# A two-layer hybrid mixer on one core: the scheduler orders the engines by its plain instruction model in place of a played time line

## The chip, the core and the metric

The kernel runs on one core of a Trainium2 chip. The core has five engines that work at the same time, each through its own list of instructions in the order in which the list stands: TensorE (PE; its weight loads are shown apart as PEld), VectorE (DVE), ScalarE (ACT), GpSimd (POOL) and SyncE (SP), which here issues all transfers. An instruction that needs another engine's result waits for a semaphore, and everything behind it on its engine waits with it. The metric is the device time of one execution in microseconds, less is better.

## The reference

Two layers over 1024 latent and 256 context tokens of width 1024. Each layer projects the normed tokens with one wide matrix into the inputs of three mixers, runs the mixers, and projects their outputs back:

```python
h = rms_norm(x) * (1 + scale[:, None]) + shift[:, None]
hc = rms_norm(ctx) * (1 + scale_c) + shift_c
aq, ak, av, ag, xbc, dtr, z, rq, rk, rv, rg = split_columns(h @ w_in, IN_SPLITS)
...
q_l = apply_rope(attn_heads(aq, attn_q_norm), cos, sin)
k_l = apply_rope(attn_heads(ak, attn_k_norm), cos, sin)
...
s = jnp.einsum('bqhmd,bkhmd->bhmqk', q, k).astype(jnp.float32) * (ATT_QK_DIM ** -0.5)
p = jax.nn.softmax(s, axis=-1)
a = p[:, :, 0] - lam * p[:, :, 1]
...
ys_l, _, _ = bidirectional_scan(cm_l, bm_l, vf_l, vb_l, laf_l, lab_l, ssd_sf, ssd_sb, True)
yr_l, _, _ = bidirectional_scan(q_rl, k_rl, v_rl, v_rl, lf_rl, lb_rl, ret_sf, ret_sb, True)
...
mix = jnp.concatenate([attn_lat, ssd_lat, ret_lat], axis=-1).astype(x.dtype)
x_new = x + gate[:, None] * (mix @ w_out)
```

The mixers are differential attention (4 heads, two softmaxes each), a state-space scan in both directions (16 heads) and a retention scan in both directions (4 heads). The last layer gives the latent tokens alone.

## The kernel before

**The work.** Tokens lie in three chunks (512, 512, 256). Each product with a projection matrix is taken in three parts (high times high, high times low, low times high) of numbers that ACT rounds (L282) and DVE or POOL subtracts (L284). Such a product over the depth of 1024 is a group of 24 matmuls into one bank of PSUM: `t_group` at L310 (weights first) or `dense_n` at L312 (tokens first). These dense groups are the filler of the kernel. The mixers are the rest: `dt_chunk` makes the time steps of the scan for a chunk of tokens (PE's L578, L625 to L628 and L648, with DVE, ACT and POOL between them), `pair_prep` and `pair_phase` run the scan for two heads at a time (L766, L772, L793 to L834), `pair_end` gates a pair (POOL's L895, ACT's L897), `head_prep` norms and rotates the queries and keys of a head, `head_loop` runs its attention, one iteration for 128 queries, and `ret_mix` is the retention.

**The rope.** `qk_norm` ends with a product on DVE (L942) and one on POOL (L943). `rope` then works in two halves: POOL multiplies by the sines (L924) into a side tile rm, DVE multiplies by the cosines in place (L925), so it must not begin before POOL has read, and adds the crossed terms (L928, L929):

```python
nc.gpsimd.tensor_tensor(out=m, in0=x4, in1=sb, op=ALU.mult)
nc.vector.tensor_tensor(out=x4, in0=x4, in1=cb, op=ALU.mult)
```

**An iteration of attention.** `head_b` makes the scores s of one softmax on PE (L986, two matmuls a chunk of keys, three chunks), their maxima mx on DVE (L988, and nb over the three at L993), and the exponentials e with their sums z on ACT (L998). It runs twice. `head_c1` adds up z (zs, L1007), takes its reciprocal (rz, L1011) and the ratio rho (L1013), and subtracts the second softmax from the first in place (e, L1016). PE transposes the result (L149, t<-ident,e), DVE or ACT copies it out (aT, L118 or L116), and PE multiplies by v (L1037). The scores have three banks of PSUM, so a score pair waits until the exponential of the pair three before it has been read.

**What sets the order.** The Python code writes the instructions down in one sequence. Generators mix the mixers' steps and the dense groups: `pump` takes one step of the stream of dense groups, `phase` does so between two steps of a mixer until a budget (`SHARE`) is used. That sequence is only a preference. On leaving the `TileContext`, its scheduler plays the program against a model of the chip, and at each moment gives an engine the earliest written instruction among those that are ready by the model. What comes out is the fixed list of each engine, with the semaphores. Which matmul fills the gap until a transpose is ready is thus decided by how long the model thinks that the engines between take. The argument `schedule_with_timeline_sim` picks the model.

## Time and profile before

| | |
|---|---|
| median of 3 runs | 2871.17 us (2867.28 to 2872.06) |
| the profiled execution | 2869.1 us |
| its span, first to last instruction | 2867.3 us |
| PE busy | 2665.5 us, 17116 matmuls |
| DVE, ACT, POOL busy | 1781.3, 1056.4, 772.1 us |
| mean granted clock of TensorE | 0.964 |
| the chain that ended last | PE 76%, DVE 12%, ACT 3% of the span |

Busy time is that of an engine's own instructions; the rest of the span it waits or has nothing to do. The chain is followed back from the last instruction, at each step to what released it. The granted clock is a share of TensorE's full 2.4 GHz; the chip grants this or half of it.

### The profile page before, as it was taken

How to read it: one execution, taken by the hardware profiler on the slowest of the kernel's cores; microseconds unless marked ns; L12 is line 12 of the kernel's file. 1: busy time of each engine (PE TensorE's matmuls, PEld its weight loads, DVE VectorE, ACT ScalarE, POOL GpSimd, SP SyncE). 2: the span in 40 equal slices, each digit the busy share in tenths (PEclk: the TensorE clock that was granted, in tenths of full speed). 3: DMA queues.
4: the chain of work that ended last, by engine and by line, in shares of the span. 5: the costliest groups of instructions: out<-in, count | busy, mean ns of one | idle time of the engine just before them, and what ended most of it. 6: DMA issues, size and time to landing. Idle time of an engine off the chain costs nothing.

```text
span 2867.3 us, 45100 instructions
## 1 busy us (share of the span) xinstructions
PE 2665.5 (93%) x17116; PEld 2339.0 (82%) x17116; DVE 1781.3 (62%) x4213; ACT 1056.4 (37%) x2678; POOL 772.1 (27%) x688
## 2 busy tenths in 40 slices
PE   6799999999999999989989989999999999999999
PEld 4578877888888899977878777878988888889787
DVE  5567767656677766565435566667676767564651
ACT  3443333224454545341223443332254444442330
POOL 2333223232111121243331423223421221022540
PEclk9899999999999999998999999999999999999999
DMA  6021212222111111033452112112210010002461
GB/s 244 10 62 62 67 44 83 70 69 89 45 54 45 54 31 39 27 110 109 136 179 95 36 41 72 53 50 65 60 30 16 23 30 23 23 17 66 139 209 55
DMA packets 111832, 196.04 MB, mean 68 GB/s; under 512 B 13600, under 2 KB 43104, under 8 KB 111616
## 3 DMA queue, kind: packets, MB, share of 16 engines
q1 hardware_dynamic: 111616, 193.17, 21.3%
q8 instruction: 135, 2.21, 0.3%
q14 instruction: 81, 0.66, 0.1%
HBM read 155.43 MB, written 37.68 MB: 67 GB/s over the span
## 4 chain that ended last, share of the span: by engine, by line
PE 76%; DVE 12%; ACT 3%; issue 2%; DMA 2%; POOL 1%; SPq 0%; DVEq 0%; ACTq 0%; POOLq 0%
PE mm L310 34%; PE mm L312 18%; PE t L149 5%; PE o L1037 4%; PE s L986 4%; PE s L772 2%; PE s L822 2%; DVE mx L988 2%; PE o L815 2%; PE t L793 1%; ACT e L998 1%; DVE e L1016 1%; DMA mr<-mix 1%; DVE rs L1156 1%; PE s L1146 1%
## 5 line engine op out<-in xcount | busy, mean ns | idle before, releaser
L310 PE MATMUL mm<-ah,wh 128*128 128x512 f32 (+1 forms) x1680 | 629.4, 375 | 30.1 <-DVE xr L1223 13.8
L310 PE MATMUL mm<-al,wh 128*128 128x512 f32 (+1 forms) x1680 | 622.8, 371 | 1.5 <-DVE al L284 0.9
L310 PE MATMUL mm<-ah,wl 128*128 128x512 f32 (+1 forms) x1680 | 622.4, 371 | 0.6 <-POOL wl L284 0.6
L284 POOL TENSOR_TENSOR wl<-raw,wh 128x512 fp32r<-128x512 f32 x224 | 294.5, 1335 | 769.5 <-ACT wh L282 736.9
L312 PE MATMUL mm<-wh,ah 128*128 128x256 f32 x1568 | 455.7, 291 | 9.5 <-DVE q L118 7.0
L312 PE MATMUL mm<-wl,ah 128*128 128x256 f32 x1568 | 450.4, 287 | 0.0
L312 PE MATMUL mm<-wh,al 128*128 128x256 f32 x1568 | 448.7, 286 | 0.0
L310 PEld LDWEIGHTS mm<-ah,wh 128*128 128x128 f32 x1680 | 322.3, 192 | 85.8 <-issue 13.8
L310 PEld LDWEIGHTS mm<-al,wh 128*128 128x128 f32 x1680 | 322.2, 192 | 51.1 <-issue 1.4
L310 PEld LDWEIGHTS mm<-ah,wl 128*128 128x128 f32 x1680 | 321.2, 191 | 51.2 <-POOL wl L284 1.1
L312 PEld LDWEIGHTS mm<-wh,ah 128*128 128x128 f32 x1568 | 302.5, 193 | 16.6 <-DVE q L118 7.7
L998 ACT ACTIVATE e<-s,nb 128x512 f32<-128x512 f32 (+1 forms) x384 | 231.7, 613 | 206.2 <-DVE nb L993 203.6
L312 PEld LDWEIGHTS mm<-wl,ah 128*128 128x128 f32 x1568 | 302.7, 193 | 2.4 <-POOL wl L284 0.2
L312 PEld LDWEIGHTS mm<-wh,al 128*128 128x128 f32 x1568 | 302.3, 193 | 2.2 <-issue 0.2
L988 DVE TENSOR_REDUCE mx<-s 128x1 f32<-128x512 f32 (+1 forms) x400 | 225.1, 589 | 55.4 <-PE s L986 53.2
L986 PE MATMUL s<-kT,qT 128*128 128x512 f32 (+1 forms) x800 | 215.8, 375 | 17.0 <-ACT e L998 15.5
L282 ACT ACTIVATE wh<-raw 128x512 fp32r<-128x512 f32 x224 | 130.0, 625 | 226.2 <-PE mm L310 103.9
L1037 PE MATMUL o<-v,aT 128*128 128x128 f32 x1312 | 174.9, 276 | 0.0
L986 PEld LDWEIGHTS s<-kT,qT 128*128 128x128 f32 x800 | 134.3, 193 | 41.3 <-ACT e L998 26.5
L1037 PEld LDWEIGHTS o<-v,aT 128*128 128x128 f32 x1312 | 163.8, 193 | 4.1 <-DVE v L118 0.8
L794 ACT ACTIVATE t<-t 128x512 f32<-128x512 f32 x144 | 82.2, 582 | 146.5 <-PE t L793 142.5
L766 POOL TENSOR_TENSOR xw<-xn,dtpk 128x512 f32<-128x512 f32 (+2 forms) x96 | 79.4, 838 | 208.9 <-PE s L772 93.5
(282 smaller groups left out, 4544.5 us busy)
## 6 DMA issues: line engine op xcount, KB each, us to landing
raw<-in_wi_dram SPq DMA_DIRECT2D x176, 256.0 KB
wa<-in_wa_dram SPq DMA_DIRECT2D x48, 512.0 KB
E<-cume SPq DMA_DIRECT2D x144, 128.0 KB
mr<-mix SPq DMA_DIRECT2D x64, 256.0 KB
raw<-in_wo_dram SPq DMA_DIRECT2D x32, 256.0 KB
x<-xr SPq DMA_DIRECT2D x26, 256.0 KB
mix<-cv SPq DMA_DIRECT2D x8, 640.0 KB
mix<-sg SPq DMA_DIRECT2D x8, 640.0 KB
```

The lines of the kernel that those rows point to most:

```text
L149: self.nc.tensor.transpose(ps[:, j * P:(j + 1) * P], srcs[i + j], self.ident)
L282: nc.scalar.activation(out=hi, in_=x, func=AF.Copy)
L284: e.tensor_tensor(out=lo, in0=x, in1=hi.bitcast(F32), op=ALU.subtract)
L310: nc.tensor.matmul(ps, lhsT=w, rhs=x, start=st, stop=sp)
L312: nc.tensor.matmul(ps, lhsT=x, rhs=w, start=st, stop=sp)
L766: nc.gpsimd.tensor_tensor(out=xw, in0=xn[:, a:a + m].rearrange("p t (h e) -> p t h e", h=2), in1=self.wend[:, a:a + m, h0:h0 + 2].unsqueez ...
L772: nc.tensor.matmul(ps[:, j * P:(j + 1) * P], lhsT=bn[:, c, :], rhs=xw[:, j].rearrange("p h e -> p (h e)"), start=True, stop=True)
L794: nc.scalar.activation(out=ps, in_=ps, func=AF.Exp)
L986: nc.tensor.matmul(ps[:, 0:n], lhsT=qT[:, 2 * m + s, :], rhs=kT[m][:, t0:t0 + n], start=(s == 0), stop=(s == 1))
L988: nc.vector.tensor_reduce(out=mx[:, ci:ci + 1], in_=ps[:, 0:n], axis=AX.X, op=ALU.max, negate=len(chunks) == 1)
L998: nc.scalar.activation(out=em[:, t0:t0 + n], in_=pss[ci][:, 0:n], func=AF.Exp, bias=nb, accum_out=z[:, 3 * m + ci:3 * m + ci + 1])
L1037: nc.tensor.matmul(po[:, 0:P], lhsT=aT[j], rhs=v[:, j, :], start=(j == b0), stop=(j == NT - 1))
```

## The change

```diff
-    with _tile.TileContext(nc, schedule_with_timeline_sim=True) as tc:
+    with _tile.TileContext(nc, schedule_with_timeline_sim=False) as tc:
```

The program that goes in is the same, and so is every instruction that comes out; only their order on each engine and the semaphores between them differ. PE's list has 12287 rows before and 12322 after, where equal neighbours are merged, and nearly all of it is shifted a little. Three places follow. Names carry the number of the tile, so that the same tile can be found in both.

The first place is on DVE, in the second head of the first layer, where the queries of the next head are rotated (q2_1212_7414) while an iteration of attention runs (s_1453_8512 and its neighbours are scores, e_1422_8357 the exponentials that the transposes wait for). Before:

```order
L942 TENSOR_TENSOR q2_1212_7414<-q2_1212_7414,ry_1414_8327 128x1280
L1007 TENSOR_REDUCE zs_1458_8530<-z_1416_8341 128x2
L1011 RECIPROCAL rz_1459_8532<-zs_1458_8530 128x2
L1013 SCALAR_TENSOR_TENSOR rho_1460_8534<-zs_1458_8530,nlam0_280,rz_1459_8532 128x1
L1016 SCALAR_TENSOR_TENSOR e_1422_8357<-e_1445_8455,rho_1460_8534,e_1422_8357 128x1280
L118 COPY v3_1429_8383<-mm_1461_8537 128x128
L988 TENSOR_REDUCE mx_1452_8511<-s_1453_8512 128x1
L988 TENSOR_REDUCE mx_1452_8511<-s_1454_8516 128x1
L988 TENSOR_REDUCE mx_1452_8511<-s_1455_8520 128x1
L993 TENSOR_REDUCE nb_1456_8524<-mx_1452_8511 128x1
L925 TENSOR_TENSOR q2_1212_7414<-q2_1212_7414,cos_338 128x512
L118 COPY v3_1429_8383<-mm_1477_8612 128x128
```

After:

```order
L942 TENSOR_TENSOR q2_1212_7414<-q2_1212_7414,ry_1414_8327 128x1280
L993 TENSOR_REDUCE nb_1444_8453<-mx_1440_8440 128x1
L1038 TENSOR_SCALAR O_1195_7358<-o_1447_8486,rz_1424_8363 128x128
L988 TENSOR_REDUCE mx_1452_8511<-s_1453_8512 128x1
L925 TENSOR_TENSOR q2_1212_7414<-q2_1212_7414,cos_338 128x512 x2
L928 TENSOR_TENSOR q2_1212_7414<-q2_1212_7414,rm_1449_8500 128x8x32
L929 TENSOR_TENSOR q2_1212_7414<-q2_1212_7414,rm_1449_8500 128x8x32
L928 TENSOR_TENSOR q2_1212_7414<-q2_1212_7414,rm_1450_8505 128x8x32
L929 TENSOR_TENSOR q2_1212_7414<-q2_1212_7414,rm_1450_8505 128x8x32
L988 TENSOR_REDUCE mx_1452_8511<-s_1454_8516 128x1
L988 TENSOR_REDUCE mx_1452_8511<-s_1455_8520 128x1
L1007 TENSOR_REDUCE zs_1458_8530<-z_1416_8341 128x2
```

Both products by the cosines (L925) and the four L928 and L929 have moved ahead of two of the three maxima (L988); nb, the ratio rho and e follow behind the maxima, where before e stood ahead of all of this.

The second place is on PE, an iteration later: the transposes of e_1457_8526 (t_1488_8695). Rows of L312 are dense matmuls. Before, the score s_1495_8715 stands 23 dense matmuls and another score ahead of the transposes; these are the last rows ahead of them:

```order
L312 MATMUL mm_1508_8780<-wh_1397_8272,al_111_567 128x256
L986 MATMUL s_1502_8764<-kT_991_6388,qT_1469_8586 128x256 x2
L312 MATMUL mm_1508_8780<-wh_1397_8272,ah_110_566 128x256
L312 MATMUL mm_1508_8780<-wl_1398_8273,ah_110_566 128x256
L312 MATMUL mm_1508_8780<-wh_1397_8272,al_111_567 128x256
L312 MATMUL mm_1508_8780<-wh_1397_8272,ah_110_566 128x256
L312 MATMUL mm_1508_8780<-wl_1398_8273,ah_110_566 128x256
L312 MATMUL mm_1508_8780<-wh_1397_8272,al_111_567 128x256
L312 MATMUL mm_1508_8780<-wh_1397_8272,ah_110_566 128x256
L149 MATMUL t_1488_8695<-ident_87,e_1457_8526 128x128 x4
```

After, from that score on:

```order
L986 MATMUL s_1495_8715<-kT_1026_6530,qT_1438_8433 128x256 x2
L312 MATMUL mm_1499_8735<-wh_1397_8272,ah_110_566 128x256
L312 MATMUL mm_1499_8735<-wl_1398_8273,ah_110_566 128x256
L312 MATMUL mm_1499_8735<-wh_1397_8272,al_111_567 128x256
L312 MATMUL mm_1499_8735<-wh_1397_8272,ah_110_566 128x256
L312 MATMUL mm_1499_8735<-wl_1398_8273,ah_110_566 128x256
L312 MATMUL mm_1499_8735<-wh_1397_8272,al_111_567 128x256
L312 MATMUL mm_1499_8735<-wh_1397_8272,ah_110_566 128x256
L312 MATMUL mm_1499_8735<-wl_1398_8273,ah_110_566 128x256
L149 MATMUL t_1488_8695<-ident_87,e_1457_8526 128x128 x4
L149 MATMUL t_1490_8702<-ident_87,e_1457_8526 128x128 x4
```

The transposes have moved up to 8 dense matmuls behind the score s_1495_8715, and the score s_1502_8764 has moved behind them.

The third place is on PE at the start of the layer, where the log decays la_174_1104 of the third chunk come from POOL (L617). Between the transposes of L578 that begin this chunk's time steps and L625, which reads la, 81 dense matmuls stand before and 44 after; in the other five chunks it is 72 to 91 before and 34 to 49 after. The last rows after the change:

```order
L310 MATMUL mm_182_1139<-ah_149_858,wl_65_352 128x256
L310 MATMUL mm_182_1139<-ah_149_858,wh_64_351 128x256
L310 MATMUL mm_182_1139<-al_150_859,wh_64_351 128x256
L625 MATMUL s_175_1109<-la_174_1104,uf_341 128x32
L626 MATMUL s_175_1109<-la_174_1104,ub_342 128x32
L628 MATMUL t_176_1112<-la_174_1104,ones_89 128x64
L310 MATMUL mm_182_1139<-ah_149_858,wl_65_352 128x256
L310 MATMUL mm_182_1139<-ah_149_858,wh_64_351 128x256
```

L625 has moved from the middle of a later dense group (mm_195_1216) into the group mm_182_1139.

## Rows read from the trace of the kernel before

**Rows 1.** Page, part 1: busy time, share of the span, instructions.
```profile
PE 2665.5 (93%) x17116; PEld 2339.0 (82%) x17116; DVE 1781.3 (62%) x4213; ACT 1056.4 (37%) x2678; POOL 772.1 (27%) x688
```

**Rows 2.** Cores: span and mean granted clock of TensorE.
```profile
core 0: 2867.3 us, clock 0.964
```

**Rows 3.** PE's waits: what waits, for what; us in total, times, longest.
```profile
PE s L986 <- ACT e L998: 15.5, 15, 2.2
...
PE t L149 <- DVE khl L284: 11.1, 10, 2.9
PE t L149 <- DVE cv L512: 7.8, 4, 2.4
PE t L149 <- DVE e L1016: 7.4, 6, 2.1
PE t L793 <- DVE mt L796: 7.4, 6, 2.3
PE s L772 <- POOL xw L766: 7.2, 5, 2.4
```

**Rows 4.** A stretch of attention by windows: us busy of each engine (x instructions).
```profile
800.00:900.00 100.00, 92.83 (x715) 85.32 (x713) 78.84 (x187) 49.68 (x154) 17.79 (x10) 0.98 0.12 39
```

**Rows 5.** Timeline of DVE, 866 to 892 us: start, us, line, operation.
```profile
873.09 1.49 DVE L942 TENSOR_TENSOR q<-q,ry 128x1280 f32<-128x1280 f32 x1
...
874.89 2.81 DVE L1013 SCALAR_TENSOR_TENSOR rho<-zs,nlam,rz 128x1 f32<-128x1 f32 x1
877.74 2.66 DVE L1016 SCALAR_TENSOR_TENSOR e<-e,rho,e 128x1280 f32<-128x1280 f32 x1
...
880.52 1.60 DVE L988 TENSOR_REDUCE mx<-s 128x1 f32<-128x512 f32 x3
...
882.24 0.68 DVE L925 TENSOR_TENSOR q<-q,cos 128x512 f32<-128x512 f32 x1
...
883.63 0.41 DVE L928 TENSOR_TENSOR q<-q,rm 128x256 f32<-128x256 f32 x1
883.97 0.42 DVE L929 TENSOR_TENSOR q<-q,rm 128x256 f32<-128x256 f32 x1
...
890.79 0.22 DVE L1013 SCALAR_TENSOR_TENSOR rho<-zs,nlam,rz 128x1 f32<-128x1 f32 x1
891.05 1.55 DVE L1016 SCALAR_TENSOR_TENSOR e<-e,rho,e 128x1280 f32<-128x1280 f32 x1
```

**Rows 6.** Timeline of POOL, 864 to 900 us, all of its rows.
```profile
874.73 2.95 POOL L943 TENSOR_TENSOR q<-q,keep 128x1280 f32<-128x1280 f32 x1 [35.53 <-DVE zs L1007]
877.76 3.77 POOL L924 TENSOR_TENSOR rm<-q,sin 128x512 f32<-128x512 f32 x2
```

**Rows 7.** Timeline of ACT, 872 to 892 us.
```profile
889.01 0.68 ACT L998 ACTIVATE e<-s,nb 128x512 f32<-128x512 f32 x1
```

**Rows 8.** Timeline of PE, 875 to 896 us; idle time before in brackets.
```profile
879.08 0.28 PE L312 MATMUL mm<-wl,ah 128*128 128x256 f32 x1
879.20 0.28 PE L312 MATMUL mm<-wh,al 128*128 128x256 f32 x1
880.45 1.09 PE L149 MATMUL t<-ident,e 128*128 128x128 f32 x8 [0.98 <-DVE e L1016]
...
894.16 1.04 PE L149 MATMUL t<-ident,e 128*128 128x128 f32 x8
```

**Rows 9.** Line L924: ns least, median, most; first and last start.
```profile
L924 POOL TENSOR_TENSOR rm<-k,sin x16: 1266/1287/1343, 576.5 to 2359.7; 128x512 f32<-128x512 f32 x16
```

**Rows 10.** Line L1016, the same columns.
```profile
L1016 DVE SCALAR_TENSOR_TENSOR e<-e,rho,e x72: 476/1551/2668, 647.5 to 2559.1; 128x1280 f32<-128x1280 f32 x64, 128x256 f32<-128x256 f32 x8
```

**Rows 11.** Timeline of PE, 142.5 to 152.9 us.
```profile
144.91 0.28 PE L310 MATMUL mm<-al,wh 128*128 128x256 f32 x1
```

**Rows 12.** Timeline of POOL, 138 to 152 us.
```profile
147.41 0.34 POOL L617 TENSOR_TENSOR la<-dtw,keep 128x64 f32<-128x64 f32 x1
```

**Rows 13.** Line L895, columns as in rows 9.
```profile
L895 POOL TENSOR_TENSOR cv<-cv,zu x16: 2357/2902/3324, 228.7 to 2040.5; 128x1280 f32<-128x1280 f32 x8, 128x1024 f32<-128x1024 f32 x8
```

## Prediction

> **What bounds the kernel now.** I read the engines' shares first [rows 1]: TensorE is busy 2665.5 of 2867.3 us, 93%, so idle for 2867.3 - 2665.5 = 202 us. No other engine is near that, and the work is the same after the change, instruction for instruction. So the question is only whether PE's 202 us of idle time grow or shrink. Second comes the clock [rows 2]: the mean granted clock is 0.964, so 0.036 x 2867.3 = 103 us of PE's time is the price of stretches at 1.2 instead of 2.4 GHz; that is 103 / 202 = 0.51 us beside each idle us. I use it as a factor of 1.51 on every us that PE stands more or less, though not each short wait brings a slow stretch. Third, the list of PE's waits [rows 3]: the mixer's own waits, where a score, a transpose or a decay matmul stood a little too early, are the six largest that the order can move. They sum to 15.5 + 11.1 + 7.8 + 7.4 + 7.4 + 7.2 = 56 us over the whole kernel, so in the old order the filler matmuls cover nearly every chain. Last, a stretch of attention [rows 4]: PE is busy 93 of 100 us and DVE 79, so DVE is the second bound there, and it takes its instructions strictly as they stand.
>
> **What moves, and its price.** In the new PE order the mixer's matmuls stand earlier against the dense ones (L310, L312), and the dense ones stand together in whole groups of 24. I lay the new order on the old durations at three places and count them up.
>
> *The rope, first place (ordered rows of DVE above).* L925 needs POOL's L924, which needs POOL's L943, which needs DVE's L942. In the old order DVE does rho, e and three maxima (L1013, L1016, L988) between L942 and L925, and finds POOL ready. In the new order both L925 and the four L928/L929 stand right behind the first maximum, and behind them wait the other two maxima, nb, rho and e. L942 ends at 874.58 [rows 5]. POOL's L943 then takes 2.95 us, to 877.68; one L924 takes 1.29 (the median) [rows 6, 9], so the second one ends at about 880.3. L925 takes 0.68 [rows 5], four additions start 0.34 apart behind it, so DVE comes back to the maxima at about 882.3; two of them (three take 1.60 in [rows 5]) end at 883.4, and zs, a copy and nb, small ones like the 0.22 of L1013 that overlap in part, give nb at about 883.9, and the first exponential (0.68 [rows 7]) ends at 884.6. PE's next score pair waits for that one to free its bank (s_8594). Before them stand three score pairs, the last released by the third exponential of the pair before (its nb now stands right behind L942, and three exponentials of at most 0.68 that overlap end about 1.9 later, at 876.5), and 39 dense matmuls at 0.12 us each [rows 8], so PE is there at 876.9 + 4.7 = 881.6 and stands 3.0 us. The old order stood 0.98 us in that place [rows 8], so the net is 2.0. There are 16 such ropes in the attention heads (32 L924 on q and k, of which [rows 9] show the 16 on k; two in a rope): 16 x 2.0 = 32 us. Bounds: all 16 lose 3.0, 48 us; or none does and the 0.98 goes too, -16.
>
> At this place the old trace shows a second thing. L1013 makes one element for each partition and took 2.81 us, ending at 877.70 just when POOL's L943 ended (877.68); the same line took 0.22 us at 890.79, after the last of POOL's work in this stretch [rows 5, 6]. L1016 behind it took 2.66 instead of 1.55: together 3.7 us longer, more than the 3.0 that the new place costs. The Trainium skill ("SBUF — State Buffer", "Who interferes with whom") says that a VectorE instruction with two SBUF inputs shares an interface with GpSimd and that the second to issue waits for the whole of the first; the trace agrees. By that rule the new order gives back what the old one lost here, since DVE now stands still while POOL works, and the rope term would be 0 instead of 32. This is the second rival below.
>
> *The attention's transposes, second place (ordered rows of PE above).* t_8695 needs e_8526 from L1016. The old order has 23 dense matmuls and a score between s_8715 and it, and it started at 894.16 without a wait [rows 8]. The new one has 8 dense matmuls. s_8715 is released by the second exponential, at 889.01 + 0.68 = 889.7 [rows 7]; 0.24 us of score and 8 x 0.12 us later PE is there, at 890.9. e_8526 was ready at 891.05 + 1.55 = 892.6 [rows 5], so PE stands 1.7 us. L1016 runs 72 times [rows 10]. At the rope's place its transposes stand behind 39 dense matmuls and lose nothing of their own, so I take one iteration in four: 18 x 1.7 = 31 us, between 0 and 72 x 1.7 = 122.
>
> *The time steps of the state-space part (dt_chunk).* L625 needs POOL's L617. Between L578 and L625 stand 72 to 91 dense matmuls in the six chunks before, and 34 to 49 after; in the third chunk 81 and 44 (24 of one group and 20 of the next). The 44th ended at 144.91 + 0.28 = 145.2; L617 ended at 147.41 + 0.34 = 147.75 [rows 11, 12]. PE stands 2.6 us. Six chunks: 16 us, from 0 to 16, since the chunks differ in what covers them.
>
> *The gate's square (L897).* ACT waits there for POOL's L895, 2.9 us a time, 16 times [rows 13], and evacuations of dense groups (L485) now stand behind it. PE has up to a dense group in hand (24 matmuls, 2.9 us), so I take 1.0 us of the 2.9 each: 16 us, from 0 to 46.
>
> *What it gives back.* Groups of dense matmuls in one piece, and mixer chains that start sooner, take away part of the 56 us of [rows 3]: half, -28, from 0 to -56.
>
> Sum: 32 + 31 + 16 + 16 - 28 = 67 us, with the clock 67 x 1.51 = 101. The profiled execution took 2869.1 us (span 2867.3), 2 below the median of the three runs, so 2869.1 + 101 = **2970 us**.
>
> **The rivals.** *Every iteration waits.* If the tight place is in all 72 iterations, because DVE is at 79% and its head of line now blocks more, the second term is 122 instead of 31: 158 x 1.51 = 239, 3108 us. For it: [rows 4]; against it: the whole groups of 24 behind each cluster let the chain catch up.
>
> *The rope is free* (the shared interface, above): 35 x 1.51 = 53, 2922 us. For it the 2.81 us of [rows 5]; against it that not DVE's time counts but when nb comes, 883.9.
>
> *Faster.* The mixer's earlier places take away all of the 56 us, and DVE and ACT, whose orders move along with PE's, have the results there sooner than the old times say, so that of the losses only the time steps' 16 us stay: -40 x 1.51 = -60, 2809 us. It decides below 56 / 72 = 0.8 us for each L1016, all losses put together. For it: the chains by their bare durations fit the new gaps in most iterations; against it: both places that I worked out in attention miss by 1.7 to 3.0 us.
>
> *Nothing.* The moves are local, and groups of 24 matmuls (2.9 us) take up each loss: 2869 us within 6 us (0.2%, about what a measurement of this kernel tells from no change).
>
> **How the numbers follow.** Forecast 0.49, every iteration waits 0.20, free rope 0.17, faster 0.09, nothing 0.05. All but the last two are slower by over 0.2%: slower 0.86, same 0.05, faster 0.09. The likeliest case alone is 2923 to 3017 us (its first two terms at half and at one and a half times their size). The range of 8 in 10 takes in the free rope at 2922 with room for a smaller second term, 2885, and the case in which every iteration waits, 3108, 3120; what lies outside is the faster case, nothing, and the sum of all upper bounds.
>
> **What the new profile would show.** Right: PE's idle time near 270 us, not 202; L925 waiting for POOL L924 in the list of DVE's waits with 20 to 50 us, where the old trace has 1.5 us; PE's transposes of e (L149) waiting for L1016 with some 30 us instead of 7.4; L625 waiting for POOL la; and a mean clock near 0.95. Wrong: if L925 waits and PE's scores do not, the rope is free; if the clock stays at 0.964 while idle time grows, the factor 1.51 was wrong; if PE's largest new wait is on a DMA, or on a dense group's evacuation, the loss is one that I have not priced.

## The result and the profile after

The changed kernel takes 2912.51 us in the median of 4 runs (2908.22 to 2918.20), the kernel before 2870.86 in the same comparison: a ratio of 1.0149, 95% interval 1.0132 to 1.0167. It is 42 us slower. The prediction was 2970 us, 101 slower, in a range from 2885 to 3120.

The page of the kernel after (part 1), its cores view and its list of PE's waits (what waits, for what; us in total, times, longest):

```profile
PE 2696.2 (92%) x17116; PEld 2345.6 (80%) x17116; DVE 1767.3 (61%) x4213; ACT 1067.4 (37%) x2678; POOL 764.6 (26%) x688
```

```profile
core 0: 2916.4 us, clock 0.958
```

```profile
PE s L986 <- ACT e L998: 16.2, 7, 3.1
PE mm L312 <- DVE q L118: 14.4, 3, 6.4
PE t L149 <- DVE cv L512: 13.4, 6, 5.6
...
PE s L625 <- POOL la L617: 10.6, 3, 4.4
...
PE t L149 <- DVE sg L1099: 7.4, 2, 5.3
...
PE s L772 <- POOL xw L766: 4.7, 7, 2.1
...
PE t L149 <- DVE e L1016: 2.5, 2, 1.3
...
PE t L793 <- DVE mt L796: 2.0, 3, 1.0
...
PE t L149 <- DVE khl L284: 0.6, 1, 0.6
```

PE is idle for 2916.4 - 2696.2 = 220 us, where it was 202 [rows 1], and the clock takes (1 - 0.958) x 2916.4 = 122 us, where it took 103 [rows 2]. The profiled execution's 49 us (2916.4 - 2867.3) are thus 18 us of idle time, 19 us of slow clock and 12 us in which PE counts as busy at full speed for a little longer. (This execution is the slowest of the four; the others have a clock of 0.958 to 0.963, and the medians lie 42 us apart.) In the list of waits [rows 3], the transposes of e have fallen from 7.4 to 2.5 us and those of khl from 11.1 to 0.6; the scores stay at 16, but in 7 waits of up to 3.1 us instead of 15 of up to 2.2. What has grown are waits for L118, which empties banks of dense groups, and for L512 (7.8 before); the one for L1099 is new. The largest of L118 was 7.0 us before, in three waits as well:

```profile
PE mm L312 <- DVE q L118: 7.0, 3, 5.7
```

Where the time went is read at places at which both orders have done the same matmuls. The windows of the two kernels between such places (columns as in [rows 4]; the count of PE's matmuls tells that the work is the same within 2), before and then after:

```profile
0.00:555.40 555.40, 493.19 (x2923) 405.92 (x2924) 354.06 (x908) 198.53 (x383) 168.10 (x163) 0.93 0.24 79
555.40:666.50 111.10, 105.20 (x786) 95.27 (x785) 63.60 (x146) 35.79 (x91) 32.99 (x20) 0.97 0.28 91
666.50:1213.70 547.20, 522.40 (x3854) 478.09 (x3855) 376.41 (x906) 247.75 (x756) 105.37 (x78) 0.99 0.14 45
1213.70:1994.30 780.60, 718.82 (x4075) 613.53 (x4074) 465.31 (x1072) 251.58 (x526) 239.86 (x243) 0.94 0.28 86
1994.30:2075.50 81.20, 81.20 (x643) 77.44 (x642) 46.06 (x118) 24.42 (x58) 34.45 (x23) 1.00 0.21 63
2075.50:2548.00 472.50, 436.55 (x3074) 400.27 (x3072) 321.50 (x763) 222.12 (x669) 81.99 (x54) 0.98 0.08 24
2548.00:2867.30 319.30, 308.17 (x1770) 268.48 (x1770) 154.35 (x304) 76.18 (x197) 109.31 (x108) 0.99 0.33 106
```

```profile
0.00:547.90 547.90, 490.00 (x2923) 402.77 (x2924) 347.16 (x894) 199.59 (x383) 167.46 (x163) 0.93 0.25 81
547.90:673.80 125.90, 112.94 (x787) 101.41 (x786) 72.63 (x175) 36.12 (x91) 38.22 (x22) 0.91 0.24 80
673.80:1234.10 560.30, 531.60 (x3854) 480.90 (x3852) 368.00 (x891) 251.90 (x756) 94.89 (x77) 0.98 0.14 43
1234.10:2019.90 785.80, 723.34 (x4077) 607.29 (x4076) 450.09 (x1072) 254.46 (x527) 240.57 (x244) 0.96 0.28 86
2019.90:2116.00 96.10, 86.41 (x643) 81.12 (x642) 52.18 (x119) 23.21 (x56) 32.06 (x21) 0.95 0.16 48
2116.00:2567.40 451.40, 433.48 (x3076) 395.91 (x3075) 321.30 (x768) 226.06 (x674) 82.43 (x54) 0.98 0.09 26
2567.40:2916.40 349.00, 318.48 (x1770) 276.18 (x1768) 155.93 (x296) 76.05 (x194) 108.98 (x108) 0.96 0.30 97
```

The seven stretches are the start with the scan of the first layer, the preparation of its first attention head, its iterations of attention, the change of layers with the second scan, then head and iterations again, and the end (retention and projection). After minus before they are -7.5, **+14.8**, +13.1, +5.2, **+14.9**, -21.1 and **+29.7** us. PE's idle time (length minus busy time) moves by -4.3, +7.1, +3.9, +0.7, +9.7, -18.0 and +19.4. The iterations of attention, on which 63 of the prediction's 95 us of losses (before what it gives back) rested, come out 8 us shorter. The net loss lies at the three stretches, of 96 to 349 us, in which the work changes from one mixer to the next.

DVE and ACT waited as foreseen. The list of waits of DVE has L925 for L924 with 29.4 us (1.5 before, the last of the three lines), that of ACT L897 for L895 with 43.1 (11.8 before):

```profile
DVE q L925 <- POOL rm L924: 18.3, 7, 3.7
...
DVE k L925 <- POOL rm L924: 11.1, 4, 4.3
```

```profile
DVE q L925 <- POOL rm L924: 1.5, 1, 1.5
```

```profile
ACT zu L897 <- POOL cv L895: 43.1, 16, 4.3
```

### The profile page after: what moved, and what is told of

Its sections match the earlier page's. It is cut to its first block, busy times and chain, and to the rows that moved or that the text cites. A ratio compares the mean times of both kernels' runs of the same rounds, so it can differ in the third digit from the quotient of the medians.

```text
span 2916.4 us, 45079 instructions
## 1 busy us (share of the span) xinstructions
PE 2696.2 (92%) x17116; PEld 2345.6 (80%) x17116; DVE 1767.3 (61%) x4213; ACT 1067.4 (37%) x2678; POOL 764.6 (26%) x688
## 5 line engine op out<-in xcount | busy, mean ns | idle before, releaser
L310 PE MATMUL mm<-ah,wh 128*128 128x512 f32 (+1 forms) x1680 | 638.1, 380 | 31.5 <-DVE xr L1223 11.9
L310 PE MATMUL mm<-al,wh 128*128 128x512 f32 (+1 forms) x1680 | 631.5, 376 | 3.3 <-POOL al L284 2.9
L310 PE MATMUL mm<-ah,wl 128*128 128x512 f32 (+1 forms) x1680 | 629.2, 375 | 1.8 <-POOL wl L284 1.8
L284 POOL TENSOR_TENSOR wl<-raw,wh 128x512 fp32r<-128x512 f32 x224 | 297.6, 1348 | 1039.2 <-ACT wh L282 1038.5
L312 PE MATMUL mm<-wh,ah 128*128 128x256 f32 x1568 | 459.7, 293 | 32.4 <-DVE q L118 14.4
L312 PE MATMUL mm<-wl,ah 128*128 128x256 f32 x1568 | 453.0, 289 | 2.1 <-POOL wl L284 2.1
L312 PE MATMUL mm<-wh,al 128*128 128x256 f32 x1568 | 453.0, 289 | 0.0
L312 PEld LDWEIGHTS mm<-wh,ah 128*128 128x128 f32 x1568 | 307.3, 196 | 37.9 <-DVE q L118 15.0
L312 PEld LDWEIGHTS mm<-wl,ah 128*128 128x128 f32 x1568 | 307.6, 196 | 3.7 <-POOL wl L284 2.7
L312 PEld LDWEIGHTS mm<-wh,al 128*128 128x128 f32 x1568 | 307.2, 196 | 0.8 <-issue 0.2
L988 DVE TENSOR_REDUCE mx<-s 128x1 f32<-128x512 f32 (+1 forms) x400 | 225.7, 588 | 56.3 <-PE s L986 55.3
L986 PE MATMUL s<-kT,qT 128*128 128x512 f32 (+1 forms) x800 | 212.0, 380 | 16.6 <-ACT e L998 16.2
L986 PEld LDWEIGHTS s<-kT,qT 128*128 128x128 f32 x800 | 138.2, 196 | 43.1 <-ACT e L998 21.4
L1037 PE MATMUL o<-v,aT 128*128 128x128 f32 x1312 | 165.1, 275 | 0.0
L1037 PEld LDWEIGHTS o<-v,aT 128*128 128x128 f32 x1312 | 157.1, 192 | 2.4 <-ACT e L998 0.8
```

What stands on the lines that cost most here:

```text
L284: e.tensor_tensor(out=lo, in0=x, in1=hi.bitcast(F32), op=ALU.subtract)
L310: nc.tensor.matmul(ps, lhsT=w, rhs=x, start=st, stop=sp)
L312: nc.tensor.matmul(ps, lhsT=x, rhs=w, start=st, stop=sp)
L986: nc.tensor.matmul(ps[:, 0:n], lhsT=qT[:, 2 * m + s, :], rhs=kT[m][:, t0:t0 + n], start=(s == 0), stop=(s == 1))
L988: nc.vector.tensor_reduce(out=mx[:, ci:ci + 1], in_=ps[:, 0:n], axis=AX.X, op=ALU.max, negate=len(chunks) == 1)
L1037: nc.tensor.matmul(po[:, 0:P], lhsT=aT[j], rhs=v[:, j, :], start=(j == b0), stop=(j == NT - 1))
```

## The experiments

All kernels are made with one tool. The scheduler runs with its plain model, and each instruction of an engine is tied behind its predecessor in a written list by an ordering edge, which costs no semaphore. With the lists of the new order the program after comes out (all_new below); the old lists were not run alone, but the order on PE and ACT in the trace of old_rope_fwd is that of the kernel before. Any mixture of both can be run. Theory A is the prediction's own account, theory B the reading of the windows above; C and D, on what happens at the places, are told in the expectations that use them. Each kernel was timed beside the kernel before on its chip, but not all on one chip. Across chips the ratios to the kernel before are the safer comparison, and each holds to 4 to 7 us either way.

```diff
+def _pin(nc, tc):
...
+            if prev is not None and x:
+                tc.add_manual_dep(by[name], prev, mb.DependencyInfo(mb.DependencyClass.NoSync, mb.DependencyReason.DATA),
+                                  reason="pin")
...
-    with _tile.TileContext(nc, schedule_with_timeline_sim=True) as tc:
+    with _tile.TileContext(nc, schedule_with_timeline_sim=False) as tc:
         tile_hybrid_kernel(tc, args, out)
+        _pin(nc, tc)
```

**The yardstick: all lists new.**

> The new order of every engine, written out as pins: the kernel after, as a yardstick on the same chip for the other three. Every theory: 2912 within 6 us.

Measured 2913.55 us, ratio to before 1.0139 (1.0116 to 1.0163). The edges cost nothing that these runs can tell, and the 42 us come from the order alone.

### Which stretch loses

The lists change source at the places above ("until" in the time of the source's own profile):

```diff
+new_start: new until 548, then old
+new_entry: old until 555.4, new until 673.8, old until 1994.3, new until 2116, then old
+new_loop:  old until 666.5, new until 1234.1, old until 2075.5, new until 2567.4, then old
+new_rest:  old until 1213.7, new until 2019.9, old until 2548, then new
```

> The new order on all engines up to 548 us (its own time; start, conditioning, time steps and the first scan pairs), the old order from there on. Theory A (the prediction: dt_chunk and the gate's square cost in the scans): half of the 16 + 16 us of these terms, times 1.51, about +15 to +24 us. Theory B (read off the two traces by places where both orders have done the same matmuls: the loss sits in stretches where the work changes from one mixer to the next): -7 us here, 2864.

> The new order only in the two stretches in which the first attention head of a layer is prepared (548 to 674 and 2020 to 2116 us of the new trace), the old order elsewhere. Theory A: these stretches hold two or three of the 16 ropes and none of the iterations, so +5 us or less. Theory B: +14.8 + 14.9, about +30 us, 2900.

> The new order only in the iterations of attention (674 to 1234 and 2116 to 2567 us of the new trace), the old order elsewhere. Theory A: the ropes and the transposes of e are here, 63 us of idle time, 95 us with the clock; even scaled down to the loss that was measured it must be most of the 42 us, 2895 to 2965. Theory B: +13 - 21, about -8 us, 2863.

> The new order from the end of the first layer's attention to the second layer's last scan pair (1234 to 2020 us of the new trace) and from 2567 us to the end (retention, output projection), the old order elsewhere. Theory A: the other half of the time steps' and the gate's terms, +15 to +24 us, all of it before 2020 us. Theory B: +5 there and +30 from 2567 us to the end, about +35 us, 2906.

| | median, us (before 2870.58) | ratio, 95% interval | difference |
|---|---|---|---|
| new_start | 2861.27 | 0.9963 (0.9951 to 0.9976) | -9 |
| new_entry | 2903.85 | 1.0117 (1.0099 to 1.0135) | +33 |
| new_loop | 2859.84 | 0.9965 (0.9952 to 0.9979) | -11 |
| new_rest | 2912.67 | 1.0145 (1.0126 to 1.0163) | +42 |

Theory A falls: the iterations of attention are faster in the new order, and so are the start's time steps and scan. Theory B holds in sign at all four and in size within 7 us (new_rest has 42 instead of 35, with an interval that begins at 36). (The four add up to 55, 13 more than the whole loss; which of them has too much was not found out.)

### What loses there

At these stretches PE waits for a bank of PSUM, or for a transpose's input, that DVE has not come to yet. The clearest place is the retention's chain of states, 18 products (L1156), nine in each direction, each of which needs the one before it in its direction. In the old order two to six other instructions stand inside seven of the eight such chains, in the new one none. Timeline of the kernel after, DVE from 2603 to 2617 us, then POOL and PE in the same stretch:

```profile
2605.41 9.60 DVE L1156 SCALAR_TENSOR_TENSOR rs<-rs,retc,rst 64x128 f32<-64x128 f32 x18 [3.35 <-ACT rst L116]
2615.04 0.49 DVE L118 COPY rk<-mm 128x128 f32<-128x128 f32 x2
```

```profile
2610.29 3.81 POOL L284 TENSOR_TENSOR wl<-raw,wh 128x512 fp32r<-128x512 f32 x3 [22.72 <-ACT wh L282]
```

```profile
2615.39 0.58 PE L312 MATMUL mm<-wh,ah 128*128 128x256 f32 x1 [4.92 <-DVE rk L118]
```

A dense group (L312) wants a bank whose evacuation, L118 with 0.28 us, stands behind 9.60 us of chain; PE stands 4.92 us. The view of the line L1156 gives the rest (ns least, median, most):

```profile
L1156 DVE SCALAR_TENSOR_TENSOR rs<-rs,retc,rst x144: 342/351/1368, 1213.3 to 2770.2; 64x128 f32<-64x128 f32 x144
```

At the median of 0.351 us the 18 products would have taken 6.3 us; the missing 3.3 fall in the time of POOL's three splits (L284) of 1.27 us each: three of the products, one beside each split, take 1.37, 1.23 and 1.24 us.

First trial: five instructions move, in two of the eight chains.

```diff
 L1156 (5th of 18)
+L118 rk<-mm
 L1156 (6th to 13th)
+L118 rk<-mm
 L1156 (14th to 18th)
-L118 rk<-mm
-L118 rk<-mm
...
 L1156 (11th of 18)
+L1223 xr<-mm
 L1156
+L1099 sg<-t
 L1156
+L1099 sg<-t
 L1156 (14th to 18th)
-L1223 xr<-mm
-L1099 sg<-t
-L1099 sg<-t
```

> The whole new order, but in two of the eight chains of 18 state products of the retention (L1156, DVE) the instructions that stand behind the chain are put into it: two evacuations of dense groups (L118, rk) in the chain at 2605 us, L1223 and two L1099 in the one at 2760 us; five instructions move. Theory C: the two waits of 4.9 and 5.3 us go, with half of the slow stretches behind them (6.8 + 10.2 us), 19 us, 2894. Theory D: 2906 to 2918.

Measured 2900.35 us (ratio to before 1.0103, 1.0077 to 1.0129), 10 to 13 us less than the order after, by the ratios or the medians: halfway between the theories' numbers, and not much more than the two intervals leave open. The traces give 7 us in the stretch of the retention (all_new 348.9, open_chain 341.5). Both theories have a part in it. In the trace of open_chain the wait of 4.9 us is gone altogether (C); in place of the one of 5.3 PE stands 0.5, 1.1 and 2.2 us at the next three results (D).

Second trial, in the two preparations of a first head: the evacuations go ahead of the rope, of the splits of k (L284) and, on ACT, of the gate's square (L897). DVE in the first one:

```diff
+L118 q<-mm
 L925 k<-k,cos
 L928 k<-k,rm
+L118 q<-mm
 L929 k<-k,rm
 L925 k<-k,cos
 L928 k<-k,rm
-L118 q<-mm
 L929 k<-k,rm
+L118 q<-mm
 L284 khl<-k,khl x6
-L118 q<-mm x2
```

> The whole new order, but in the two stretches where the first head of a layer is prepared six evacuations of dense groups (L118, q and v) on DVE, and the four on ACT (L116) that lead them, stand ahead of the rope, the splits of k and the gate's square instead of behind them; nothing else moves. Theory C (the loss is a bank of PSUM that PE wants and whose evacuation stands behind a long run of other work on DVE or ACT): the three waits of 6.4, 4.9 and 2.2 us go, and half of the slow-clock stretches behind them (10.2 + 6.8 + 3.4 us), 24 us in all, 2889. Theory D (PE's own order asks for the mixer's results too early, whatever DVE does; PE will stand a few instructions later instead): 2906 to 2918.

Measured 2898.53 us (1.0099, 1.0074 to 1.0125), 11 to 15 less (11 in the two stretches of the traces): C at about half of its number. The wait of 4.9 us is gone; that of 6.4 has become one of 4.0 for the next bank, and that of 2.2 is followed by one of 3.6 for kT, where 1.3 stood before. This trial does not turn the change back: in the old order, too, five of the six evacuations on DVE stand behind the rope and three of them behind most of the splits of k, and PE stood 5.7 us for a q's L118 in the first entry. What it finds is, at this place, a better order than both.

Third trial, the prediction's first term: eight ropes go back behind nb (of the fifth only its first L925 has to move). In the profile after, PE stands at each of these eight places, for 3.0, 3.1, 2.4, 3.1, 1.6, 3.0, 3.1 and 3.1 us. The place that the prediction worked out is the third. DVE and PE there:

```profile
876.95 1.49 DVE L942 TENSOR_TENSOR q<-q,ry 128x1280 f32<-128x1280 f32 x1
...
882.94 2.37 DVE L925 TENSOR_TENSOR q<-q,cos 128x512 f32<-128x512 f32 x2 [1.85 <-POOL rm L924]
...
886.57 1.01 DVE L988 TENSOR_REDUCE mx<-s 128x1 f32<-128x512 f32 x2
...
887.57 0.28 DVE L118 COPY v<-mm 128x128 f32<-128x128 f32 x1
887.77 0.14 DVE L993 TENSOR_REDUCE nb<-mx 128x1 f32<-128x3 f32 x1
...
888.01 0.22 DVE L1013 SCALAR_TENSOR_TENSOR rho<-zs,nlam,rz 128x1 f32<-128x1 f32 x1
888.27 1.55 DVE L1016 SCALAR_TENSOR_TENSOR e<-e,rho,e 128x1280 f32<-128x1280 f32 x1
```

```profile
887.90 0.39 PE L312 MATMUL mm<-wh,ah 128*128 128x256 f32 x1 [2.42 <-DVE nb L993]
```

The view puts this wait down to nb, which ends last, at 887.91; the matmul does not read nb, and the copy L118 that empties a dense group's bank ends at 887.85.

```diff
 L988 mx<-s
-L925 q<-q,cos x2
-L928, L929, L928, L929 q<-q,rm
 L988 mx<-s x2
 L1007 zs<-z
 L118 v<-mm
 L993 nb<-mx
+L925 q<-q,cos x2
+L928, L929, L928, L929 q<-q,rm
 L1011 rz<-zs
```

> The whole new order, but at the eight ropes of the attention iterations where the profile after shows DVE standing at L925 for POOL's L924 (1.85 to 2.86 us each, 19 us together), the six DVE instructions of the rope stand behind the next nb (L993), as in the old order; nothing else moves. Theory A (the prediction's rope term: PE's scores wait while DVE stands): 8 x 2.0 to 2.9 us x 1.51 = 24 to 34 us back, 2878 to 2888. Theory C (PE has dense matmuls in hand there, so that DVE's stand costs nothing): 2912 within 6 us.

Measured 2892.44 us (1.0083, 1.0060 to 1.0107), 16 to 21 less than after (16 in the iterations of the traces, against all_new). C stands in this expectation for the view that in the iterations dense matmuls cover whatever is late on DVE. It was mine and falls; A is right in kind and comes out below its number. Why not all of the 22 us of stands and the slow clock behind them comes back is seen in the list of PE's waits of rope_back:

```profile
PE t L149 <- DVE e L1016: 15.6, 9, 3.2
...
PE s L986 <- ACT e L998: 2.2, 2, 1.6
```

The scores' waits fall from 16.2 to 2.2 us, and those of the transposes of e rise from 2.5 to 15.6: without the stand at the rope PE comes to the transposes sooner. The two are one chain, and the loss is to be counted once.

The same term the other way round: the old order, with five ropes put forward.

```diff
 L942 q<-q,ry
 L988 mx<-s
+L925, L928, L929, L925, L928, L929 of q
...
-L925, L928, L929, L925, L928, L929 of q
```

> The old order, but five ropes of the attention iterations (two on k, three on q, the one of the prediction's first place among them) stand on DVE right behind the first maximum (L988) after L942, as in the new order. Theory A, the prediction's price: 5 x 2.0 x 1.51 = +15 us, 2886. By what the eight ropes gave back in the new order, 2.5 us each: +12, 2883. Theory C (PE has dense matmuls in hand in the old order): 2871 within 5.

Measured 2910.85 us (1.0131, 1.0106 to 1.0156): +37, 7.4 us for each rope, well over all three expectations. The list of PE's waits of this kernel:

```profile
PE s L986 <- ACT e L998: 28.2, 16, 5.9
...
PE mm L312 <- DVE v L118: 8.0, 1, 8.0
```

One stand for a bank (L118 v) is 8.0 us long. But this is not the new order's move: the five are all among the eight, and four of them stand a single instruction behind L942 here, where the new order has three to five between. At three of these four the nb of an earlier softmax, which the new order has ahead of the rope, now stands behind it, and PE's longest stands for a score, 5.5 and 5.9 us, are at two of them. DVE stands 3.3 to 4.1 us at each of the four, against 1.85 to 2.86 at the eight places in the new order:

```profile
DVE k L925 <- POOL rm L924: 8.0, 2, 4.1
DVE q L925 <- POOL rm L924: 6.6, 2, 3.3
```

So ropes put forward cost time under the old order of PE too. Why it is 7.4 us for a rope here and 2 to 2.6 (16 to 21 over eight) in the new order, whether by PE's list or by these earlier places, no run tells apart.

Last, the three trials together:

> The new order with the three sets of moved instructions together (the eight ropes behind nb, the six evacuations and their four partners on ACT at the entries, the five instructions in two chains of the retention). If the three waits are separate, the differences to the kernel after add up: 20 + 14 + 12 = 46, 2866, about the time of the old order. If one stall takes over what another gives up: 2880 to 2895.

Measured 2870.89 us, ratio to before 0.9996 (0.9980 to 1.0012), against 2913.55 for the whole new order on the same chip. The gains add up: 41 to 43 us, where 46 were expected. 58 instructions of DVE and ACT moved (43 of the ropes, 10 of the entries, 5 of the chains) are worth as much as the whole net loss; PE's order is that of the kernel after, to the last matmul.

That does not make them its whole cause. The stretches of all3, cut at the same matmuls (the two entries, the second layer's iterations, the end):

```profile
547.15:668.96 121.81, 111.22 (x786) 100.59 (x785) 68.78 (x175) 35.87 (x91) 35.90 (x21) 0.93 0.26 82
...
1999.88:2089.74 89.86, 85.02 (x643) 80.13 (x642) 50.94 (x119) 23.41 (x57) 32.13 (x21) 0.96 0.18 51
2089.74:2530.67 440.93, 427.40 (x3076) 390.15 (x3074) 317.80 (x768) 226.05 (x674) 82.46 (x54) 1.00 0.09 26
2530.67:2871.60 340.93, 318.36 (x1770) 275.50 (x1768) 154.76 (x296) 76.11 (x194) 108.22 (x108) 0.96 0.31 99
```

The two entries and the end are still 10.7, 8.7 and 21.6 us longer than in the kernel before. Of the 59 us that they lost, 18 have come back, and 41 are not explained by a trial. The total is level because the iterations of both layers are 29 us shorter than before, and the start 8. In the end's list of waits the largest left are 4.4 us for L1176 and 3.8 and 2.7 for L1090; nothing was run on these.

### A mixture that beats both

```diff
+best1: new until 548, old until 2075.5, new until 2567.4, then old
+best2: best1, and the three ropes of the second stretch behind nb
```

> The new order up to 548 us and in the second layer's attention iterations (2116 to 2567 us of the new trace), the old order elsewhere. If stretches add up (theory B): the start gained 8 us and the second layer's iterations 24 us in the traces of the kernels that had these alone, 2871 - 32 = 2839 us, faster than both orders. If the two stretches only moved slow-clock time about: 2855 to 2865.

> The faster mixture (new order to 548 us and in the second layer's attention, old elsewhere: 2837 measured) with the three ropes of that attention stretch put behind nb. If the ropes cost there what they gave back in the whole new order (20 us for eight): 2837 - 7 = 2830. If they are covered there: 2837 within 5.

best1 takes 2836.87 us (0.9886, 0.9861 to 0.9911), best2 2828.89 (0.9843, 0.9818 to 0.9869). Stretches add up, and the ropes give back 8 us there too by the medians (12 by the ratios, 7 in that stretch of the traces). The page of best2, part 1:

```profile
PE 2653.9 (94%) x17116; PEld 2328.1 (82%) x17116; DVE 1769.7 (63%) x4213; ACT 1059.3 (37%) x2678; POOL 773.6 (27%) x688
```

PE is idle for 2831.4 - 2653.9 = 177.5 us.

## Why the prediction was wrong

The direction was right and the size was not: 42 us instead of 101, inside the wide range (2885 to 3120) but below the 2923 to 3017 of the likeliest case. The direction was right in part by luck: the iterations of attention, where the sum put most of the loss, are 8 us faster, and the net loss lies at stretches that the sum left out.

The steps that failed are the transposes of e, which overlap with the rope and were counted as a second loss; the rope's number of places, 16 instead of 8; the gate's square, which held up no evacuation of L485 that PE waited for; and the changes of mixer, put at nothing by leaving them out.

Of the signs that it named, L925's 29 us lie within 20 to 50, L625 waits and the clock is at 0.958; but PE's idle time is 220 us and not 270, and the transposes of e wait 2.5 us and not 30. One of its signs of being wrong came: PE's waits for evacuations of dense groups (L118) are among the largest new ones. Term by term, in us of PE's idle time:

- **The rope, +32.** The mechanism was right, also in its numbers: nb was to come 883.9 - 874.58 = 9.3 us behind the end of L942 and came 887.91 - 878.44 = 9.5 behind it; PE was to stand 3.0 us and stood 2.4 there, 3.0 or 3.1 at six of the other seven places. (The 0.98 us that it set against this was another wait, of the transposes for e.) The number of places was wrong: I took 16 ropes from one that I had laid out, and in the trace eight stand like it. What waited was in three of the eight cases, the worked one among them, not a score but a dense group's bank (L312), since L118 stood behind the rope too (at 887.57 in the timeline above); I had not listed it. The trial prices the term at 16 to 21 us with the clock, where the prediction had 32 x 1.51 = 48.
- **The transposes of e, +31.** This step failed outright. "One iteration in four" was laid on the old times of DVE, one iteration behind a place at which PE had just been said to stand 3 us; after such a stand e is ready. The waits fell to 2.5 us, and rope_back shows the two taking each other's place. Forecast as two terms, they were one.
- **The time steps, +16.** L625 waits 10.6 us, in three waits, and L648 2.8 (3.1 before); the size was about two thirds of the term. The start as a whole still gained 9 us (new_start), while the waits of L541 there (18.8 us before, among them 9.8 for L492 and 7.0 for L456) have fallen to 1.5, and PE's idle time there is 4.3 us less; these waits were not in my list, and no run takes the start apart.
- **The gate's square, +16.** ACT waits 43.1 us there (11.8 before), and no wait of PE for the evacuations of L485 is in the list: 0. It is not shown to be free: at the second entry (2065 to 2068 us) evacuations of q (ACT's L116) stand behind such a wait of 3.5 us, shortly before PE's stand of 4.9 us for q's L118. evac_entry moved both engines' evacuations at once and does not part the two.
- **What it gives back, -28.** The six rows of [rows 3] went from 56.4 to 39.4, so -17, though the scores' row holds new waits now.
- **What was not in the sum.** The three short stretches: +7.1 + 9.7 + 19.4 = 36 us of idle time, twice the net. I had looked at the three kinds of place that repeat, and not at the changes of mixer. The trials took back 18 of the 59 us there (above); what the other 41 are stays open.
- **The clock, 1.51.** 18 us of idle time came with 19 of slow clock and 12 of longer busy time, 2.7 us in all for each; from the kernel before to best2, 24 us less idle time came with 36 us less span, 1.5 for each. The factor is not settled by these; with the higher one the forecast would have been further out.

Of the rivals, the free rope at 2922 us has the nearest number and the wrong reason. DVE did get back what POOL cost it: L1013 and L1016 take 0.22 and 1.55 us at that place now, where they took 2.81 and 2.66 [rows 5]. PE lost its 2.4 us all the same, as the prediction's objection had it, and rope_back shows that ropes at this place are not free. "Every iteration waits" is refuted by the stretch of -21.1 us, "nothing" by the interval, and "faster" comes true in two of seven stretches, by which mechanism is open.

What stays open: why the second layer's attention gains 18 us of idle time and the first layer's loses 4. The waits that vanish in the second are those for khl, nb, e and aT; no run takes them apart.

## What to carry to other kernels

When an order changes everywhere, cut the program at places where both orders have done the same work, and price the stretches, also those where one kind of work ends and the next begins: here three such stretches lost 59 us, while the iterations of attention, in which eight ropes cost 16 to 21, still gained 8. A long run of dependent small instructions, or one that waits for a slow engine, should not stand ahead of an evacuation on an in-order engine: 58 instructions moved were worth 42 us here, though not all of them undo what the change did. A table of pinned orders makes each stretch of a schedule an experiment of its own, and the best schedule may be a mixture.

## What the runs showed of the hardware

I had not expected what POOL's work does to DVE's smallest instructions, of 8 elements for each partition. DVE and POOL of the kernel after, 2716 to 2722 us:

```profile
2717.35 0.17 DVE L132 TENSOR_TENSOR ru<-ry 128x8 f32<-128x8 f32 x1
2717.55 1.14 DVE L133 SCALAR_TENSOR_TENSOR ru<-ru,ms 128x8 f32<-128x8 f32 x1
2718.72 1.19 DVE L134 SCALAR_TENSOR_TENSOR ry<-ru,ry 128x8 f32<-128x8 f32 x1
2719.94 1.19 DVE L132 TENSOR_TENSOR ru<-ry 128x8 f32<-128x8 f32 x1
...
2721.57 0.69 DVE L1090 TENSOR_TENSOR rO<-rO,ry 128x512 f32<-128x512 f32 x1
```

```profile
2717.37 3.73 POOL L284 TENSOR_TENSOR wl<-raw,wh 128x512 fp32r<-128x512 f32 x3 [3.10 <-ACT wh L282]
```

L133, L134 and L132 take 0.17 us alone, and 1.14 to 1.19 while POOL's three splits run at 1.24 us each: one small instruction of DVE for each of POOL. The Trainium skill ("SBUF — State Buffer", "Who interferes with whom") states that a DVE instruction with two inputs in SBUF contends with a GpSimd instruction that reads SBUF, and calls the ports that they share an exclusive lock; the trace agrees with it here. The three make L1090 some 3 us late, and PE's next transpose stood 4.0 us for it.
